# Hybrid decoder layer on one core: the input projection in chunks of 2, 3, 5 and 6 k-tiles, its last chunk in 24 blocks of two tiles, and more sums by transfers

## The chip, the cores and the metric

The kernel is one program on one core of a Trainium2 chip. Its time is the device time of one execution in microseconds, the median of three runs. The engines are named as the profile names them: PE multiplies, DVE and ACT do elementwise work, POOL here mostly issues transfers, and SP issues the loads of weights. [...]

## The reference, cut to what matters

```python
mod = (silu(c) @ w_mod + b_mod)                      # 6 vectors of 2048
h = rmsnorm(x, mix_pre_w) * (1 + sc_m) + sh_m        # x: 256 x 2048, float32
proj = h @ w_in                                      # 2048 x 6160: cb, cc, cx, q, k, v, r, a_lr
y_conv = cb * causal_dwconv3(cc * cx, conv_w)
o = gla_chunked(q, k, v, log_sigmoid(a_lr @ gate_w2 + gate_b) / 16)
y_gla = rmsnorm(o, gla_norm_w) * silu(r)
x = x + g_m * rmsnorm(concat(y_conv, y_gla) @ w_out, mix_post_w)
h = rmsnorm(x, ffn_pre_w) * (1 + sc_f) + sh_f
x = x + g_f * rmsnorm((silu(g) * val) @ w_down, ffn_post_w)   # g, val = split(conv3(h @ w_up))
```

All is float32 and nothing is kept from an earlier call: every weight, w_mod's 100 MB among them, is read once per execution.

## The kernel before

Each weight comes from memory as float32 into one of six `raw` tiles (`NRAW`). ACT copies it to the matmul's type (`wh`, L140) and DVE subtracts that from the original (`wl`, L145), so a product is the sum of three matmuls: high by high, high by low and low by high. There are three buffers each of `wh` and `wl`.

The input projection (`in_units`) goes over the 16 k-tiles of h in four chunks, `CHUNKS = (2, 4, 5, 5)`, because h needs the modulation vectors sc_m and sh_m, which are themselves a product with w_mod that DVE makes row by row (`mod_steps`: one L136 per k-row of w_mod, into an accumulator). While chunk i is multiplied, the modulation of chunk i+1's k-tiles is loaded and accumulated. Each chunk goes over all 48 output tiles of 128 columns in units: four tiles a unit in chunks 0 and 1, mostly three in chunks 2 and 3. Tiles 0 to 23 are cb, cc and cx, 24 to 31 are q and k, 32 to 39 v and 40 to 47 r. Tiles from 32 on (`mm_rows`, L602 to L604) have h as the loaded operand and the weights as the streamed one, the others (`mm`, L638 to L640) the reverse. Some pairs of tiles stay in PSUM from one chunk into the next (`keep`); for the others each chunk adds its part to a sum in SBUF: `evac` and `evac_rows`, a DVE addition (L477, L494) or, in the last chunk and for the names in `BY_DMA`, an ACT copy into one of three `hf` tiles (`NHF`) and then a transfer issued by POOL that adds to its destination (L475, L492).

`drive` sets the order. For unit i it issues: its `early` steps, the load and the ACT copy of unit i+2 (`prep`), the DVE subtraction of unit i+1 (`low`), the `pre` steps, the matmuls (`inner` steps between), `mid` steps, the sums of unit i-1 (`fin`, one unit late), and the `late` steps. Tables say at which unit a step goes: `MODS` the ends of the stretches over which the modulation steps are spread, `CONV`, `SILU` and `GATE` the places of the convolution, of silu(r) and of the gating. The gated linear attention of q, k and v runs inside the last chunk: nine levels (`gla_level`), one a unit from `G0` on, each with DVE differences (L763), ACT exponentials (L782, L783), DVE products (L799), PE score products (L737) and masked copies by DVE or ACT (L820, L818); then `gla_out` multiplies by v (L839 to L842), takes norms on ACT (L401), scales (L861), multiplies by silu(r) (`gated`, L868), turns the result on PE (`turn`, L874) and splits it (`weighted`, L880, and `weighted_low`). `tail` is the list of the last chunk's units followed by the 16 units of the output projection (`out_units`, 24 matmuls of 512 columns in most), whose first four units use the convolution's half and the next four the attention's.

After that come the feed-forward's two projections, which the change leaves as they are.

Of the kernel before, what the change touches and what calls it, by code (L numbers as in the profile page):

```python
# [21 lines left out]
HEADS = 4  # L22
TAU = 16.0
QS = 128.0 ** -0.5
CHUNKS = (2, 4, 5, 5)
PLAIN = ()
NMASK = 6
XRE = 5
NA = 10
G0 = 3  # L30
SQ = 1
LEAD = 2
S0 = 61
# [2 lines left out]
NBIG = 20  # L36
XLD = (4, 8)
NLD = (9, 13)
GATE = (18, 19, 20, 21)
SILU = (17, 18)  # L40
CONV = (9, 12, 13, 15)
MODS = (10, 22, 33, 48, 72)
CHUNK1 = 12
BUSY_TAIL = (12, 13, 16, 17)
BY_DMA = ("cc", "cx", "v")
F2_AT = (71, 74, 16)
FULL = ()
FULL1 = ()
FULL2 = ()
# [18 lines left out]
def spread(steps, units, last=()):  # L68

    places = [p for u in units for p in ((u.early, u.mid, u.late) if u in last else (u.early, u.mid))]  # L70
    for i, f in enumerate(steps):
        places[i * len(places) // len(steps)].append(f)
# [31 lines left out]
def layer_kernel(ctx: ExitStack, tc, x, c, w_mod, b_mod, mix_pre_w, mix_post_w, w_in, conv_w, gate_w2, gate_b,  # L104
# [14 lines left out]
    def nm(s):  # L119
        uid[0] += 1  # L120
        return f"{s}_{uid[0]}"

    def slot(shape, dt=F32):
        return big.tile(shape, dt, tag="big", name=nm("big"))
# [7 lines left out]
    def raw_tile(shape):  # L132
        return wts.tile(shape, F32, tag="raw", name=nm("raw"), bufs=NRAW)

    def stt(o, a, s, b, op0=ALU.mult, op1=ALU.add):
        nc.vector.scalar_tensor_tensor(o, a, s, b, op0=op0, op1=op1)  # L136
# [24 lines left out]
    def mod_steps(s0, n, a, w, nj, lag=0):  # L161

        accs, cur, rows = [], {}, []

        def use(j, r):
            stt(cur["acc"], r, c_act[:, j:j + 1], cur["acc"])

        def begin():  # L170
            acc = cur["acc"] = (slot([P, n, w]) if n * w <= 1024 else
                                wts.tile([P, n, w], F32, tag="macc", name=nm("macc"), bufs=2))
            accs.extend(acc[:, s, :] for s in range(n))
            nc.gpsimd.memset(acc, 0.0)
            nc.gpsimd.dma_start(acc[0:1, :, :], b_mod_v[:, s0:s0 + n, a:a + w])

        def step(j):
            if j >= KT:
                use(*rows.pop(0))
                return  # L180
            m = nj if j < KT - nj or nj < 4 else 2
            if j % m == 0:
                cur["r"] = raw_tile([P, m, n, w])
                if m == 1:
                    nc.sync.dma_start(cur["r"][:, 0, :, :], w_mod_v[:, j, s0:s0 + n, a:a + w])
                else:
                    for s in range(n):
                        nc.sync.dma_start(cur["r"][:, :, s, :], w_mod_v[:, j:j + m, s0 + s, a:a + w])
            rows.append((j, cur["r"][:, j % m, :, :]))
            if j >= lag:  # L190
                use(*rows.pop(0))

        return accs, [begin] + [lambda j=j: step(j) for j in range(KT + lag)]

    W0 = CHUNKS[0] * P
    first_acc = slot([P, 2, W0])
# [259 lines left out]
    hts, h32 = {}, {}  # L456
    hf0 = slot([P, CHUNKS[0], T])

    written, left = set(), {}

    def evac(ci, pair, ps):

        name = names[pair // 2]
        if name not in proj:
            proj[name] = slot([P, 4, T])
        dst = proj[name][:, (pair % 2) * 2:(pair % 2) * 2 + 2, :]
        if pair not in written:
            written.add(pair)
            nc.scalar.activation(dst, ps, AF.Copy, scale=QS if name == "q" else 1.0)
        elif name == "q":  # L470
            stt(dst, ps, QS, dst)
        elif ci == len(CHUNKS) - 1 and name[:-1] in BY_DMA and pair != 10:
            away_sum = hf_tile()
            nc.scalar.copy(away_sum, ps)
            nc.gpsimd.dma_start(dst, away_sum, accum_op=ALU.add)  # L475
        else:
            nc.vector.tensor_add(dst, dst, ps)  # L477

    def evac_rows(ci, tiles, t, ps):
# [7 lines left out]
        if ci == 0:  # L487
            nc.scalar.copy(dst, ps)
        elif ci == len(CHUNKS) - 1 and name[:-1] in BY_DMA:
            away_sum = hf_tile().rearrange("p a t -> p (a t)")[:, :w]  # L490
# [5 lines left out]
    def modulate_chunk(ci, ash, early=None):  # L496
# [4 lines left out]
        def at_once():  # L501

            n = CHUNKS[0]
            for kts in pairs(k0, k1):
# [50 lines left out]
    def in_units(ci):  # L555
        k0, n = bounds[ci], CHUNKS[ci]
        if ci == 0:
            groups = [tuple(range(g, g + 4)) for g in list(range(0, 24, 4)) + list(range(44, 20, -4))]
        elif ci == 1:
            groups = [tuple(range(g, g + 4)) for g in list(range(24, 48, 4)) + list(range(0, 24, 4))]  # L560
        elif ci == 2:
            groups = [tuple(range(g, g + 3)) for g in range(21, -1, -3)]
            groups += [(45, 46, 47), (42, 43, 44), (40, 41), (37, 38, 39), (34, 35, 36), (32, 33), (30, 31)]
            groups += [tuple(range(g, g + 3)) for g in (27, 24)]
        else:
            groups = [(24, 25, 26), (27, 28, 29), (30, 31), (32, 33, 34), (35, 36, 37), (38, 39)]
            for o, m in ((0, 3), (3, 3), (6, 2)):
                groups += [tuple(range(g + o, g + o + m)) for g in (8, 16, 0)]
            groups += [(40, 41, 42), (43, 44, 45), (46, 47)]

        keep = ((12, 13, 14, 15), (8, 9, 10, 11), (12, 13, 14), ())[ci]
        banks, done, begun, more = {}, {}, {}, {}
# [1 line left out]
        def unit(tiles, plain, by_parts=False):  # L574
# [72 lines left out]
            def fin():  # L647
                for p in dict.fromkeys(nt // 2 for nt in tiles):
                    done[p] = done.get(p, 0) + sum(nt // 2 == p for nt in tiles)
                    if done[p] == 2 and p not in keep:  # L650
                        evac(ci, p, banks[p])
# [238 lines left out]
    def gate_silu(g):  # L890
        for t in range(2):
            r = proj[f"r{t}"][:, g * 512:(g + 1) * 512]
            nc.scalar.activation(r, r, AF.Silu)
# [273 lines left out]
    for j in range(12, KT, 2):  # L1167
        first_load(j, 2, slot)
    load_small()
    chunks = [in_units(ci) for ci in range(len(CHUNKS))]  # L1170
    e = CHUNKS[0] * P
    rs = {}
# [34 lines left out]
    ash, products, columns = mod_columns([first_acc[:, i, :] for i in range(2)], CHUNKS[0], pre_c[:, :CHUNKS[0]], "ash0")  # L1207
# [17 lines left out]
    allin = [u for c in chunks for u in c] + owait  # L1225
# [4 lines left out]
    for ci in range(1, len(CHUNKS)):  # L1230
        n, us = CHUNKS[ci], chunks[ci - 1]
        st = {}
        st["accs"], steps = mod_steps(0, 2, bounds[ci] * P, n * P, 2 if n <= 4 else 1, 1)
        spread(steps, allin[CHUNK1 if ci == 2 else at:MODS[ci - 1]], [c[-1] for c in chunks])
        at = MODS[ci - 1]

# [15 lines left out]
    tail = chunks[-1] + owait  # L1252
    gacc, gsteps = mod_steps(2, 1, 0, 2048, 1)
    spread(gsteps, [u for i, u in enumerate(allin) if at <= i < MODS[3]], [c[-1] for c in chunks])
    load, ones_rows, rows_used = mod_rows(gacc, mix_post_w, lambda: [slot([P, 1024]) for _ in range(2)])
    r0 = 2
    owait[r0].late.append(load)
    for h in range(2):
        owait[r0 + R0 + 1].mid.append(lambda h=h, f=ones_rows: f(h))
        owait[r0 + R0 + 2].late.append(lambda h=h, f=rows_used: f(h))  # L1260
    f1, fsteps = mod_steps(3, 2, 0, 1024, 1)
    spread(fsteps, [u for i, u in enumerate(allin) if MODS[3] <= i < MODS[4] and i - ends[2] not in BUSY_TAIL])
    for place, f in seconds:
        place.append(f)
# [14 lines left out]
    levels = [-1, 0, 1, 2, 3, 4, 5, 6, 7]  # L1279
    tail[3].late.append(gla_s)  # L1280
    for i, lv in enumerate(levels):
        diff, decay, mult, products, put = gla_level(lv)
        if lv >= 0:
            tail[G0 + i].late.append(diff)
            tail[G0 + i + 1].early.append(decay)
            tail[G0 + i + 1].pre.append(mult)
        tail[G0 + i + 2].inner.append(products)
        tail[G0 + i + 2].late.append(put)
    outputs, norms, scaled, gated, turn, weighted, weighted_low = gla_out()
    GO = G0 + len(levels) + 3  # L1290
    tail[GO].early.append(outputs)
    tail[GO].late.append(norms)
    tail[GO + 1].pre.append(scaled)
    for g in range(2):
        tail[SILU[g]].late.append(lambda g=g: gate_silu(g))
    for e in range(4):
        tail[GATE[e]].pre.append(lambda e=e: gated(e))
        tail[GATE[e]].late.append(lambda e=e: turn(e))
        tail[GATE[e] + 1].pre.append(lambda e=e: weighted(e))
        tail[GATE[e] + 1].late.append(lambda e=e: weighted_low(e))  # L1300
    for i, u in enumerate(CONV):
        first, tap, second, high_part, third = conv_pair(i)
# [244 lines left out]
```

## Time and profile before

| | us |
|---|---|
| median of three runs | 1202.89 (1202.86 to 1203.3) |
| profiled execution, its own time | 1203.08 |
| its span, first to last instruction | 1201.1 |
| PE busy | 1166.5 |
| DVE busy | 939.5 |
| ACT busy | 576.7 |
| first matmul of chunk 0 / 1 / 2 / 3 | 26.0 / 68.7 / 142.9 / 232.9 |
| first matmul of the output projection | 344.7 |

The span is what the trace covers; the execution's own time lies 2.0 us above it. The granted clock of PE is 0.998 over the span. A matmul's end is modelled in this trace and overlaps the next one, so PE's pace is read from the distance between two starts. The rows by line mix several instructions that a helper issues: L136 is every scalar-times-tensor-plus-tensor, and the tiles tell them apart (`macc<-raw,c_act,macc` is a modulation row).

### The profile page before, as it was taken

What the parts mean: (1) busy time and instruction counts of PE and PEld (TensorE: products, weight loads), DVE (VectorE), ACT (ScalarE), POOL (GpSimd) and SP (SyncE); (2) the same over time, 40 slices, a digit from 0 to 9 for tenths busy, and PEclk for the clock granted to TensorE, in tenths of its full rate; (3) what the DMA queues carried; (4) which work ended last, traced back from release to release, by engine and by line L of the source; (5) the groups of instructions that cost most, each with busy time, mean ns of one, the idle gap of its engine ahead of it and who ended that gap; (6) DMA issues with size and microseconds to landing.
All of it is one profiled execution on the core that took longest, in us unless ns stands there. A gap on an engine that the chain in (4) does not pass through costs nothing.

```text
span 1201.1 us, 16724 instructions
## 1 busy us (share of the span) xinstructions
PE 1166.5 (97%) x6771; PEld 1027.6 (86%) x6771; DVE 939.5 (78%) x963; ACT 576.7 (48%) x671; POOL 47.8 (4%) x66
## 2 busy tenths in 40 slices
PE   3899999999999999999999999999999999999997
PEld 2799999999987888888888888888888888888885
DVE  6979999999999868984698979797976664545463
ACT  4663433463683556445455444544544544343442
POOL 3000110011101010000000000000000000000000
PEclk9999999999999999999999999999999999999999
DMA  9999999998899969995476777668563675555522
GB/s 340 387 361 378 331 383 393 388 330 272 240 341 372 367 248 333 378 369 212 168 260 213 258 259 249 223 243 293 201 236 140 228 263 201 185 202 184 207 73 71
DMA packets 129182, 323.62 MB, mean 269 GB/s; under 512 B 8550, under 2 KB 35894, under 8 KB 119377
## 3 DMA queue, kind: packets, MB, share of 16 engines
q1 hardware_dynamic: 124704, 312.63, 72.2%
q0 software_dynamic: 4256, 9.92, 3.0%
q8 instruction: 53, 0.87, 0.3%
q14 instruction: 25, 0.20, 0.0%
q10 hardware_dynamic: 144, 0.01, 0.0%
HBM read 315.45 MB, written 4.19 MB: 266 GB/s over the span
## 4 chain that ended last, share of the span: by engine, by line
PE 57%; issue 30%; DVE 5%; DMA 5%; ACT 1%; SPq 1%; POOL 1%; POOLq 0%; DVEq 0%; ACTq 0%
PE ps L1057 27%; PE ps L1059 14%; PE ps L913 3%; PE ps L915 3%; PE ps L914 3%; DVE wl L145 1%; DMA big<-hf 1%; PE ps L640 1%; PE ps L639 1%; DVE macc L136 1%; PE ps L638 1%; DMA raw<-in_w_mod_dram 1%; DMA big<-in_w_in_dram 1%; DMA raw<-in_w_in_dram 1%; DMA big<-in_w_mod_dram 1%
## 5 line engine op out<-in xcount | busy, mean ns | idle before, releaser
L140 ACT CAST wh<-raw 128x2048 fp32r<-128x2048 f32 (+2 forms) x200 | 366.3, 1833 | 498.3 <-PE ps L1057 187.3
L145 DVE TENSOR_TENSOR wl<-raw,wh 128x2048 fp32r<-128x2048 f32 (+2 forms) x200 | 437.4, 2190 | 144.7 <-ACT wh L140 144.6
L1057 PE MATMUL ps<-big,wh 128*128 128x512 f32 x1400 | 495.0, 399 | 0.0
L1059 PE MATMUL ps<-big,wl 128*128 128x256 f32 x1400 | 393.1, 281 | 0.0
L1057 PEld LDWEIGHTS ps<-big,wh 128*128 128x128 f32 x1400 | 263.0, 188 | 64.8
L1059 PEld LDWEIGHTS ps<-big,wl 128*128 128x128 f32 x1400 | 264.5, 189 | 0.0
L136 DVE SCALAR_TENSOR_TENSOR macc<-raw,c_act,macc 128x2048 f32<-128x2048 f32 (+1 forms) x96 | 199.3, 2076 | 4.5 <-DMA raw<-in_w_mod_dram 2.2
L913 PE MATMUL ps<-wh,big 128*128 128x512 f32 x456 | 178.4, 391 | 0.0
L915 PE MATMUL ps<-wh,big 128*128 128x512 f32 x456 | 177.5, 389 | 0.0
L914 PE MATMUL ps<-wl,big 128*128 128x512 f32 x456 | 177.5, 389 | 0.0
L640 PE MATMUL ps<-big,wl 128*128 128x256 f32 x504 | 143.3, 284 | 4.6 <-DVE wl L145 4.6
L638 PE MATMUL ps<-big,wh 128*128 128x256 f32 x504 | 143.8, 285 | 0.0
L639 PE MATMUL ps<-big,wh 128*128 128x256 f32 x504 | 142.6, 283 | 0.1
L640 PEld LDWEIGHTS ps<-big,wl 128*128 128x128 f32 x504 | 96.5, 192 | 5.9 <-DVE wl L145 5.8
L915 PEld LDWEIGHTS ps<-wh,big 128*128 128x128 f32 x456 | 85.6, 188 | 18.0
L913 PEld LDWEIGHTS ps<-wh,big 128*128 128x128 f32 x456 | 85.6, 188 | 17.9 <-issue 0.2
L914 PEld LDWEIGHTS ps<-wl,big 128*128 128x128 f32 x456 | 85.6, 188 | 17.6 <-issue 0.2
L639 PEld LDWEIGHTS ps<-big,wh 128*128 128x128 f32 x504 | 96.6, 192 | 0.3 <-DVE big L433 0.3
L638 PEld LDWEIGHTS ps<-big,wh 128*128 128x128 f32 x504 | 96.6, 192 | 0.4 <-ACT wh L140 0.3
L136 DVE SCALAR_TENSOR_TENSOR big<-big,fcw,big 128x254 f32<-128x254 f32 (+1 forms) x176 | 72.1, 475 | 0.0
L983 DVE TENSOR_TENSOR big<-big,ps 128x256 f32<-128x256 f32 x88 | 31.1, 415 | 46.5 <-ACT big L981 46.5
L604 PE MATMUL ps<-wl,big 128*128 128x384 f32 (+2 forms) x168 | 57.1, 340 | 1.2 <-DVE wl L145 1.2
(222 smaller groups left out, 914.0 us busy)
## 6 DMA issues: line engine op xcount, KB each, us to landing
raw<-in_w_up_dram SPq DMA_DIRECT2D x88, 1024.0 KB, 5.1
raw<-in_w_mod_dram SPq DMA_DIRECT2D x64, 1024.0 KB, 6.9
raw<-in_w_down_dram SPq DMA_DIRECT2D x44, 1024.0 KB, 4.8
raw<-in_w_in_dram SPq DMA_DIRECT2D x26, 960.0 KB, 8.0
raw<-in_w_mod_dram SPq DMA_DIRECT2D x32, 640.0 KB, 7.9
raw<-in_w_out_dram SPq DMA_DIRECT2D x16, 1024.0 KB, 7.5
raw<-in_w_in_dram SPq DMA_DIRECT2D x12, 1024.0 KB, 9.1
raw<-in_w_mod_dram SPq DMA_DIRECT2D x22, 512.0 KB, 8.4
```

Source lines behind the costliest of these rows:

```text
L136: nc.vector.scalar_tensor_tensor(o, a, s, b, op0=op0, op1=op1)
L140: nc.scalar.copy(hi, raw)
L145: nc.vector.tensor_sub(lo, raw, hi.bitcast(F32))
L604: nc.tensor.matmul(ps, ht[:, 0, :], w[1][:, kk, :], start=False, stop=kk == n - 1)
L638: nc.tensor.matmul(ps, w[0][:, kk, cs], ht[:, k % 2, 0, :], start=st, stop=False)
L639: nc.tensor.matmul(ps, w[0][:, kk, cs], ht[:, k % 2, 1, :], start=False, stop=False)
L640: nc.tensor.matmul(ps, w[1][:, kk, cs], ht[:, k % 2, 0, :], start=False, stop=sp)
L913: nc.tensor.matmul(ps, a[:, i, 0, ts_], w[0][:, kk, ns], start=st, stop=False)
L914: nc.tensor.matmul(ps, a[:, i, 0, ts_], w[1][:, kk, ns], start=False, stop=False)
L915: nc.tensor.matmul(ps, a[:, i, 1, ts_], w[0][:, kk, ns], start=False, stop=sp)
L1057: nc.tensor.matmul(pss[o], wh[:, kk, cs], h2[k // 2][:, k % 2, :, :], start=(first and kk == 0), stop=False)
L1059: nc.tensor.matmul(pss[o][:, 1, :], wl[:, kk, cs], h2[k // 2][:, k % 2, 0, :], start=False, stop=(last and kk == 3))
```

## The change

- `CHUNKS` becomes (2, 3, 5, 6). The modulation of chunk 1 covers three k-tiles instead of four, that of chunk 3 six instead of five.
- The last chunk goes in 24 units of two tiles (`groups`) instead of 18 units of three or two. Its order is the same: q, k and v, then cc, cx and cb by turns, then r.
- `LEVEL_AT` gives each attention level its own unit; mostly every second unit takes one. `G0` goes.
- `BY_DMA` takes cb and r too, and the exception for pair 10 goes: all sums of the last chunk except q and k go by transfer. These are 12 transfers of 256 KB and 16 of 128 KB, where there were 7, and 6 of 192 or 128 KB.
- `CONV`, `SILU`, `GATE`, `MODS`, `BUSY_TAIL` and `F2_AT` move with the units.
- The first step of the feed-forward's modulation (a memset and a small load on POOL, `f_begin`) goes two units ahead of the others.

```diff
-CHUNKS = (2, 4, 5, 5)
+CHUNKS = (2, 3, 5, 6)
-G0 = 3
-GATE = (18, 19, 20, 21)
-SILU = (17, 18)
-CONV = (9, 12, 13, 15)
-MODS = (10, 22, 33, 48, 72)
+GATE = (24, 25, 26, 27)
+SILU = (23, 24)
+CONV = (12, 15, 18, 21)
+MODS = (10, 22, 33, 50, 78)
-BUSY_TAIL = (12, 13, 16, 17)
-BY_DMA = ("cc", "cx", "v")
-F2_AT = (71, 74, 16)
+BUSY_TAIL = (13, 15, 17, 19, 22, 23)
+BY_DMA = ("cb", "cc", "cx", "v", "r")
+F2_AT = (77, 80, 16)
+LEVEL_AT = (3, 5, 7, 9, 11, 12, 14, 16, 18)
...
-        elif ci == len(CHUNKS) - 1 and name[:-1] in BY_DMA and pair != 10:
+        elif ci == len(CHUNKS) - 1 and name[:-1] in BY_DMA:
...
-            groups = [(24, 25, 26), (27, 28, 29), (30, 31), (32, 33, 34), (35, 36, 37), (38, 39)]
-            for o, m in ((0, 3), (3, 3), (6, 2)):
-                groups += [tuple(range(g + o, g + o + m)) for g in (8, 16, 0)]
-            groups += [(40, 41, 42), (43, 44, 45), (46, 47)]
+            firsts = list(range(24, 40, 2))
+            for o in range(0, 8, 2):
+                firsts += [g + o for g in (8, 16, 0)]
+            groups = [(g, g + 1) for g in firsts + list(range(40, 48, 2))]
...
-    f1, fsteps = mod_steps(3, 2, 0, 1024, 1)
+    f1, (f_begin, *fsteps) = mod_steps(3, 2, 0, 1024, 1)
+    allin[MODS[3] - 2].late.append(f_begin)
...
-            tail[G0 + i].late.append(diff)
-            tail[G0 + i + 1].early.append(decay)
-            tail[G0 + i + 1].pre.append(mult)
-        tail[G0 + i + 2].inner.append(products)
-        tail[G0 + i + 2].late.append(put)
+            tail[LEVEL_AT[i]].late.append(diff)
+            tail[LEVEL_AT[i] + 1].early.append(decay)
+            tail[LEVEL_AT[i] + 1].pre.append(mult)
+        tail[LEVEL_AT[i] + 2].inner.append(products)
+        tail[LEVEL_AT[i] + 2].late.append(put)
...
-    GO = G0 + len(levels) + 3
+    GO = LEVEL_AT[-1] + 3
```

Three places show what moves. The first is SP in the second half of chunk 0: its own weights (`in_w_in`, 2 k-tiles by 512 columns) between the modulation rows of chunk 1. Before, and then in the changed kernel:

```order
L585 DMA raw_422<-in_w_in_dram 128x2x512
L188 DMA raw_458<-in_w_mod_dram 128x2x512 x2
L585 DMA raw_462<-in_w_in_dram 128x2x512
L188 DMA raw_486<-in_w_mod_dram 128x2x512 x2
L585 DMA raw_490<-in_w_in_dram 128x2x512
```

```order
L585 DMA raw_422<-in_w_in_dram 128x2x512
L188 DMA raw_458<-in_w_mod_dram 128x2x384 x2
L585 DMA raw_462<-in_w_in_dram 128x2x512
L188 DMA raw_486<-in_w_mod_dram 128x2x384 x2
L585 DMA raw_490<-in_w_in_dram 128x2x512
```

The order is the same; the modulation rows have 384 columns instead of 512.

The second is ACT from the scaling of the attention's result to the third `wh` of the output projection, with the semaphores that each row waits for (`DMASW` counts POOL's transfers, `DMAHW` SP's loads; `big_511` and `big_513` are r, the first and the second 128 rows of it). Before:

```order
L861 ACTIVATE big_3401<-ps_3323,grs 128x256 x2
L684 CAST big_3445<-big_337 128x2x256 [waits DVE_49]
L140 CAST wh_3449<-raw_3447 128x2048 [waits DMAHW1_49,PE_49]
L893 ACT_TABLE_LOAD
L893 ACTIVATE big_511<-big_511 128x512 [waits DVE_49]
L893 ACTIVATE big_513<-big_513 128x512 [waits DVE_49]
L140 CAST wh_3495<-raw_3493 128x2048 [waits DMAHW3_49,PE_49]
L893 ACTIVATE big_511<-big_511 128x512 [waits DVE_49]
L893 ACTIVATE big_513<-big_513 128x512 [waits DVE_49]
L140 CAST wh_3543<-raw_3541 128x2048 [waits DMAHW5_49,PE_49,Activation_49]
```

And in the changed kernel:

```order
L491 COPY hf_3589<-ps_3464 128x256 [waits DMASW2_49]
L491 COPY hf_3592<-ps_3483 128x256 [waits DMASW3_49,PE_49]
L684 CAST big_3595<-big_337 128x2x256 [waits DVE_49]
L140 CAST wh_3599<-raw_3597 128x2048 [waits DMAHW1_49,PE_49]
L491 COPY hf_3641<-ps_3551 128x256 [waits DMASW4_49]
L491 COPY hf_3644<-ps_3570 128x256 [waits DMASW5_49,PE_49,Activation_49]
L893 ACT_TABLE_LOAD
L893 ACTIVATE big_511<-big_511 128x512
L893 ACTIVATE big_513<-big_513 128x512 [waits DMASW6_49]
L140 CAST wh_3652<-raw_3650 128x2048 [waits DMAHW2_49,PE_49]
L491 COPY hf_3689<-ps_3603 128x256 [waits Activation_49]
L491 COPY hf_3692<-ps_3622 128x256 [waits DMASW7_49,PE_49,Activation_49]
L893 ACTIVATE big_511<-big_511 128x512 [waits DMASW1_49]
L893 ACTIVATE big_513<-big_513 128x512 [waits DMASW2_49,DMASW0_49]
L140 CAST wh_3704<-raw_3702 128x2048 [waits DMAHW4_49,DVE_49,PE_49]
```

The four silu rows waited for DVE's additions; now copies for r stand between them, and they wait for POOL's transfers.

The third is DVE at the second and third unit of the output projection in the changed kernel (`big_3708` is the first turned piece that `weighted_low` splits, L868 is `gated`):

```order
L145 TENSOR_TENSOR wl_3706<-raw_3650,wh_3652 128x2048
L868 TENSOR_TENSOR big_3536<-big_3536,big_511 128x256
L868 TENSOR_TENSOR big_3541<-big_3541,big_513 128x256
L136 SCALAR_TENSOR_TENSOR big_3708<-ps_3697,sv,big_3708 128x256 x2
L136 SCALAR_TENSOR_TENSOR macc_2655<-raw_3744,c_act,macc_2655 128x2048
L145 TENSOR_TENSOR wl_3751<-raw_3702,wh_3704 128x2048
L868 TENSOR_TENSOR big_3536<-big_3536,big_511 128x256
```

The last row, `gated` for the third piece, stands behind a `wl` whose `wh` (`wh_3704`) is the last ACT row shown above; that part of DVE's order is as it was.

## The prediction

> **What bounds the kernel now.** I read the busy times by stage first: chunk 0, 1, 2 and 3 of the input projection, and the output projection. Columns: PE, weight loads, DVE, ACT, POOL, clock, DMA share, GB/s.
>
> ```profile
> core 0: us, PE busy (x) PEld busy (x) DVE busy (x) ACT busy (x) POOL busy (x), PEclk, DMA share, GB/s
> 26.00:68.70 42.70, 38.81 (x264) 34.55 (x265) 37.33 (x34) 30.17 (x43) 0.00 (x0) 1.00 1.05 387
> 68.70:142.90 74.20, 74.12 (x535) 69.83 (x534) 68.64 (x56) 32.11 (x28) 2.04 (x4) 1.00 0.99 354
> 142.90:232.90 90.00, 90.00 (x703) 89.93 (x701) 87.62 (x71) 32.95 (x26) 8.08 (x4) 1.00 1.04 387
> 232.90:344.70 111.80, 109.29 (x831) 106.91 (x830) 107.16 (x113) 65.27 (x107) 14.76 (x17) 1.00 0.92 295
> 344.70:440.00 95.30, 94.85 (x428) 76.91 (x427) 83.22 (x71) 43.79 (x50) 3.19 (x3) 1.00 0.94 355
> ```
>
> PE never stops for long, yet DVE is nearly as full from 69 to 345: 263.4 of 276 us. Chunk 0 alone has PE idle, and there the loads run at 387 GB/s. The change ends before 440, so at most some ten us of PE idling are to be won. Next, PE's waits, in chunk 0 (first two rows) and from 233 to 360:
>
> ```profile
> PE ps L640 <- DVE wl L145: 2.2, 2, 1.7
> PE ps L604 <- DVE wl L145: 1.2, 2, 0.6
> ...
> PE ps L640 <- DVE wl L145: 2.4, 2, 1.9
> PE ps L874 <- DVE big L868: 0.4, 1, 0.4
> ```
>
> Each is a wait for the low half of a weight, except the last (`turn` for `gated`). A wait shows less than it costs: a matmul's modelled end lies 0.28 us behind its start, and the next starts 0.12 us later.
>
> ```profile
> 265.17 0.28 PE L638 MATMUL ps<-big,wh 128*128 128x256 f32 x1
> 265.29 0.28 PE L639 MATMUL ps<-big,wh 128*128 128x256 f32 x1
> ...
> 340.15 0.33 PE L602 MATMUL ps<-wh,big 128*128 128x384 f32 x1
> 340.32 0.33 PE L603 MATMUL ps<-wh,big 128*128 128x384 f32 x1
> ...
> 344.68 0.40 PE L913 MATMUL ps<-wh,big 128*128 128x512 f32 x1
> 344.91 0.40 PE L914 MATMUL ps<-wl,big 128*128 128x512 f32 x1
> ```
>
> By starts and counts, PE's own work is 36.5 us of chunk 0's 42.7 (8 units of 24 matmuls at 0.12, 4 of 12 at 0.23, products and transposes 2.6), 107.4 of chunk 3's 111.8 (five k-tiles 85.4, 136 score products 15.2, the product with v and the gate 6.8), and nearly all of chunks 1 and 2.
>
> **The change, chunk by chunk.** A k-tile costs PE 48 x 3 x 0.12 = 17.3 us; one moves from chunk 1 to chunk 3. Narrow rows are near free: three matmuls of 256 take 0.36 us, two of 384 0.34, some 0.8 us in all.
>
> Chunk 0. Its low halves come late because the loads do:
>
> ```profile
> ACT wh L140 <- DMA raw<-in_w_in_dram: 4.8, 2, 2.8
> ...
> raw<-in_w_mod_dram SPq DMA_DIRECT2D x22, 512.0 KB, 8.4
> ```
>
> Sixteen of these 22 loads are chunk 1's modulation, 0.5 MB each; three k-tiles instead of four take away 2.1 MB, 5.4 us at 387 GB/s. The last weights of chunk 0 then land that much earlier and PE paces the chunk: 35.8 us of work (0.7 less, a tile's products and transposes) and 1.0 us of starting waits. Chunk 1 starts at 62.8 instead of 68.7: **-5.9**.
>
> Chunk 1. DVE's prices:
>
> ```profile
> L145 DVE TENSOR_TENSOR wl<-raw,wh 128x2048 fp32r<-128x2048 f32 x29 | 66.1, 2284 | 11.4 <-ACT wh L140 11.4
> L145 DVE TENSOR_TENSOR wl<-raw,wh 128x1920 fp32r<-128x1920 f32 x26 | 55.9, 2150 | 1.9 <-ACT wh L140 1.8
> L145 DVE TENSOR_TENSOR wl<-raw,wh 128x1280 fp32r<-128x1280 f32 x9 | 13.3, 1483 | 0.5 <-ACT wh L140 0.5
> L136 DVE SCALAR_TENSOR_TENSOR macc<-raw,c_act,macc 128x2048 f32<-128x2048 f32 x34 | 79.7, 2344 | 2.7 <-issue 2.2 <-DMA raw<-in_w_mod_dram 0.5
> L136 DVE SCALAR_TENSOR_TENSOR macc<-raw,c_act,macc 128x1280 f32<-128x1280 f32 x32 | 49.3, 1540 | 1.8 <-DMA raw<-in_w_mod_dram 1.7
> L477 DVE TENSOR_TENSOR big<-big,ps 128x512 f32<-128x512 f32 x28 | 18.2, 674 | 0.4 <-PE ps L640 0.4
> ...
> 341.15 1.01 DVE L494 TENSOR_TENSOR big<-big,ps 128x384 f32<-128x384 f32 x2
> L494 DVE TENSOR_TENSOR big<-big,ps 128x384 f32<-128x384 f32 x12 | 6.1, 548 | 0.0
> ```
>
> The last two rows say that neighbours overlap by 0.08 us (2 x 0.548 against 1.01), which I take off per instruction. A low half of 1536 columns, new, lies between 1.48 and 2.15; by the line through them 1.75. The chunk's list: 12 low halves 21.0, 16 modulation rows of 1280 24.6, one of 1536 (1.81 by the same line) 1.8, 16 additions 10.8, small ones 2.2, less 51 x 0.08: 56.2 us. PE needs 56.5 (74.2 - 17.3 within 0.4). Before, the same sum is 62.7 against 74.2, so DVE ran ahead. Now it has no margin, and its idle time counts (68.64 busy of 74.2: 5.6 us, mostly waits for ACT after the new h and for one raw load); I take 4.5, since loads shrink: 60.7 us, **+3.8** against PE's need of 56.9. Bounds: 56.5, PE alone, and 65.
>
> Chunk 2. Modulation rows grow from 1280 to 1536 columns, 16 x 0.27 = 4.3 us, and one row of 2048 moves on, -2.3: DVE 89.6, with the 2.4 of idle that the stage has now 92.0. PE: 90.0 + 0.7. **+2.0**; bounds +0.7 and +5, the upper for loads, which ran at 387 GB/s here already and have 2.1 MB more.
>
> Chunk 3. PE: 107.4 + 17.3 + 0.8 = 125.5. DVE: 107.2; low halves +6.8 (24 x 1.75 for 12 x 2.15 + 6 x 1.48, less overlaps); five additions of 0.67 and three of 0.55 gone, -4.3; four more modulation rows in the stretch, +9.0; together 119, with the idle of now (4.6) 123.3. The attention's levels at every second unit and the earlier `f_begin` (its wait is the 2.2 "issue" above) keep work from bunching, but the two engines are nearly equal, so I add 1.5 to PE's: 127, against 111.8 + 17.3: **-2.1**. Bounds -3.7 and +2. POOL has 28 transfers of some 0.9 us, hidden by 127 us of chunk; conv's sums have about two units of 5 us before their readers, more than a landing (below). Output projection starts at 342.5 instead of 344.7: **-2.2** so far.
>
> **The sums of r.** Here the transfers meet a reader at once. Their time from issue to landing (min, median, max), POOL's time for one issue (three figures in ns), the median for r's size, and ACT's and DVE's prices:
>
> ```profile
> DMA to landing us min/median/max: 3.9/7.0/9.4
> L492 POOL DMA_DIRECT2D big<-hf x6: 852/895/1247, 257.1 to 274.2; - x6
> ...
> big<-hf POOLq DMA_DIRECT2D x2, 128.0 KB, 7.1
> ...
> L401 ACT ACTIVATE junk<-ps 128x256 bf16<-128x256 f32 x8 | 3.1, 383 | 0.2
> L851 ACT ACT_TABLE_LOAD x1 | 1.3, 1283 | 0.0
> L861 ACT ACTIVATE big<-ps,grs 128x256 f32<-128x256 f32 x8 | 3.0, 478 | 0.0
> L491 ACT COPY hf<-ps 128x256 f32<-128x256 f32 x2 | 0.7, 362 | 3.5 <-DMA big<-hf 3.5
> L893 ACT ACTIVATE big<-big 128x512 f32<-128x512 f32 x4 | 2.3, 624 | 1.7 <-DVE big L494 1.7
> L880 ACT ACTIVATE big<-ps,sv 128x256 fp32r<-128x256 f32 x8 | 3.3, 469 | 0.0
> L140 ACT CAST wh<-raw 128x2048 fp32r<-128x2048 f32 x7 | 13.4, 1911 | 8.7 <-issue 5.5 <-PE ps L915 3.2
> L868 DVE TENSOR_TENSOR big<-big,big 128x256 f32<-128x256 f32 x8 | 3.0, 420 | 0.0
> ```
>
> Take T as the end of attention's product with v; then PE has three units (13.0 us) before the output projection, whose units take 5.5 us and 0.5 for `turn`. ACT after T: the last square sums, a table load and a root to T+3.0, conv's taps 3.9, `wh` once a buffer is free 6.3, eight scalings 9.3, then two copies of r (9.6, 10.0), which POOL issues at 9.7 and 10.6. With 7.0 they land at 16.7 and 17.6. The fourth copy in turn has no `hf` tile until 16.7; then the table load (18.4) and two silus (19.6). `gated`, 2 x 0.42, ends at 20.4; PE wants to turn at 13.0 + 5.5: 2.0 late. Behind the silus on ACT stand the next `wh` (21.5) and the last two copies of r (22.1), and the next two silus wait for those very sums: issued at 21.9 and 22.8. By then few weights have been freed to load, so I take a landing of 5.5, between 3.9 and 7.0: 28.3, silus 28.9, `wh` 30.8, `weighted` 31.6. DVE holds its order: `weighted_low` 32.4, a modulation row 34.7, `wl` 36.9, `gated` 37.7. PE is done with the third unit at 32.4: 5.4 late. Together **+7.5**, of which the 0.8 that `turn` cost before (0.4 seen, twice 0.16 hidden) goes off: +6.7. With landings of 3.9 both times the delay is 2.8, with 9.4 13. From there PE has what it had; the rest is unchanged.
>
> The Trainium skill, "DMA: Bandwidth & Descriptors", section "Anatomy of one DMA — SWDGE (gpsimd) path", gives a transfer issued by GpSimd 2.0 us plus its bytes at 436 GB/s, an estimate of 2.3 us for 128 KB. The rows here, 3.9 at least under a loaded DMA, disagree. By the rule the third `gated` would come 0.4 late and the sum be 1202.9 - 2.2 - 0.4 = 1200.3.
>
> Sum: 1203.08 - 2.2 + 6.7 = 1207.6 for the profiled execution; the median lies 0.2 below, so **1207.4**.
>
> **Rivals.** (1) *Sums land soon.* If the transfers land in the 3.9 us of the quickest one, PE is late by 2.8 rather than 7.5: 1202.9 - 2.2 + 2.0 = 1202.7, no change. For it: DMA is freer once ACT stalls. Against: the median for 128 KB is 7.1. With landings of 2 us, half the quickest row, nothing is late and the old 0.8 goes too: 1202.9 - 2.2 - 0.8 = 1199.9, faster. That is the side on which the page's rule stands.
>
> (2) *PE paces every chunk.* If DVE's idle time was slack that it could afford, chunks 1 to 3 take PE's 56.5, 90.7 and 125.5: the projection starts at 62.8 + 272.7 = 335.5, 9.2 earlier, and 1202.9 - 9.2 + 6.7 = 1200.4, faster. For it: no PE wait at all from 69 to 233 before. Against: DVE's lists equal PE's within 0.3 us in chunk 1.
>
> (3) *DVE and loads starve.* Each DVE idle keeps `raw` tiles longer, loads come later, and the idle of chunks 1 and 2 doubles, +7 against my sum: 1214. For it: both engines and the loads are all full there. Against: loads now stay back to back from 142.9 to 232.9 with DVE at 97%.
>
> **How the numbers follow.** Forecast 0.57; rival 1 0.11 with landings of 3.9 and 0.05 with 2; rival 2 0.12; rival 3 0.15. Range: the bottom takes in rivals 1 and 2, 1199.8; the top lies between the forecast and rival 3, 1212.8. About 0.2%, 2.4 us, is what a measurement here can tell: faster 0.05 + 0.12 = 0.17; same 0.11 and 0.13 of the forecast, where its terms fall small, 0.24; slower 0.44 + 0.15 = 0.59.
>
> **What would show it.** Chunk 1's first matmul near 62.8; chunk 1 lasting 60 to 61 with PE waits for L145, none of which stood there before; chunk 3's near 215.5; the output projection's near 342.5. Then ACT's L893 waiting for a transfer `big<-hf`, some 6 us in the second pair, and PE's L874 waiting for DVE L868 by 7 to 8 us in all. I am wrong if the silus wait little, or if chunk 1 lasts under 58.

## The result

The changed kernel takes 1214.7 us (median of four, 1213.45 to 1215.06) where the kernel before takes 1202.88 (1202.64 to 1203.3): a ratio of 1.0097, 95% interval 1.0082 to 1.0111, 11.8 us slower. The forecast was 1207.4 with a range up to 1212.8: the direction was right, the size too small.

First the busy times by stage of the changed kernel (chunk 0, 1, 2, 3, output projection), as the prediction showed them of the kernel before:

```profile
core 0: us, PE busy (x) PEld busy (x) DVE busy (x) ACT busy (x) POOL busy (x), PEclk, DMA share, GB/s
25.70:62.90 37.20, 36.77 (x259) 34.10 (x259) 32.89 (x35) 29.50 (x43) 0.00 (x0) 1.00 1.06 381
62.90:125.40 62.50, 58.06 (x413) 53.61 (x412) 60.20 (x55) 25.60 (x26) 2.04 (x4) 1.00 1.01 362
125.40:216.80 91.40, 91.20 (x709) 90.79 (x709) 91.22 (x71) 34.24 (x27) 6.05 (x4) 1.00 1.05 388
216.80:347.20 130.40, 126.59 (x1034) 124.92 (x1033) 118.60 (x116) 77.18 (x125) 23.35 (x27) 1.00 1.02 323
347.20:440.70 93.50, 87.17 (x386) 70.50 (x384) 70.19 (x51) 40.06 (x42) 7.48 (x9) 0.96 0.90 327
```

Two stages have PE idle where the kernel before had hardly any: chunk 1 (4.4 us) and the output projection (6.3 us, and the mean clock is 0.96 there). Chunk 3 has 3.8 us of it, in two waits, at 268 and 274.5 us, where the kernel before had 2.5. PE's waits in these three stages, one after the other (us in total, times, longest):

```profile
PE ps L640 <- DVE wl L145: 4.1, 4, 1.5
...
PE ps L640 <- DVE wl L145: 3.8, 2, 2.1
...
PE ps L874 <- DVE big L868: 6.3, 1, 6.3
```

By the first matmul of each stage, the two profiled executions stand so (us):

| | before | changed | length before | length changed | predicted |
|---|---|---|---|---|---|
| chunk 0 | 26.0 | 25.7 | | | |
| chunk 1 | 68.7 | 62.9 | 74.1 | 62.5 | 60.7 |
| chunk 2 | 142.9 | 125.4 | 90.0 | 91.5 | 92.0 |
| chunk 3 | 232.9 | 216.8 | 111.8 | 130.4 | 127 |
| output projection | 344.7 | 347.2 | 86.4 to its last unit | 93.5 | +6.7 |
| last unit of it | 431.0 | 440.7 | | | |
| last matmul of all | 1192.3 | 1202.0 | | | |
| end of span | 1201.1 | 1211.7 | 8.7 | 9.7 | 0 |

So 2.5 us are lost by the start of the output projection, 7.1 more in it, nothing in the 760 us of the feed-forward, and 1.0 behind the last matmul: 10.6, the difference of the spans. The profiled execution is the shortest of the four; the median lies 1.25 above it.

**The output projection.** DVE ahead of the wait, and PE behind it (start, duration, instruction, in brackets the idle time before it and what ended it); then the granted clock in four stretches:

```profile
365.24 0.88 DVE L136 SCALAR_TENSOR_TENSOR big<-ps,sv,big 128x256 fp32r<-128x256 f32 x2 [7.60 <-ACT big L880]
366.03 2.34 DVE L136 SCALAR_TENSOR_TENSOR macc<-raw,c_act,macc 128x2048 f32<-128x2048 f32 x1
368.29 2.29 DVE L145 TENSOR_TENSOR wl<-raw,wh 128x2048 fp32r<-128x2048 f32 x1
370.49 0.76 DVE L868 TENSOR_TENSOR big<-big,big 128x256 f32<-128x256 f32 x2
...
371.06 1.14 PE L874 MATMUL ps<-ident,big 128*128 128x128 f32 x4 [6.33 <-DVE big L868]
371.85 0.77 PE L913 MATMUL ps<-wh,big 128*128 128x512 f32 x1
372.43 0.63 PE L914 MATMUL ps<-wl,big 128*128 128x512 f32 x1
372.85 0.63 PE L915 MATMUL ps<-wh,big 128*128 128x512 f32 x1
```

```profile
360.00:366.00 6.00, 4.73 (x21) 3.57 (x19) 0.76 (x2) 4.59 (x6) 0.00 (x0) 1.00 1.06 391
366.00:371.00 5.00, 0.00 (x0) 0.00 (x0) 5.00 (x5) 3.52 (x4) 0.00 (x0) 0.63 0.30 86
371.00:372.40 1.40, 1.34 (x5) 1.22 (x6) 1.40 (x4) 0.16 (x1) 0.00 (x0) 0.50 1.02 418
372.40:374.10 1.70, 1.70 (x5) 1.32 (x4) 1.70 (x1) 0.68 (x2) 0.00 (x0) 0.50 1.06 422
```

PE wants the third turned piece at 364.6 and gets it at 371.06. Then its matmuls of 512 columns start 0.42 us apart instead of 0.23, and until 374.1 the granted clock is 0.50. The third unit of the output projection lasts 12.9 us and the fourth 7.0, against 5.94 each without the wait: 8.0 us. What DVE waited for is told by ACT and by the transfers that POOL issued from the second pair of copies:

```profile
353.75 0.63 ACT L491 COPY hf<-ps 128x256 f32<-128x256 f32 x2
360.88 0.63 ACT L893 ACTIVATE big<-big 128x512 f32<-128x512 f32 x1 [6.51 <-DMA big<-hf]
362.04 0.63 ACT L893 ACTIVATE big<-big 128x512 f32<-128x512 f32 x1 [0.52 <-DMA big<-hf]
362.58 1.89 ACT L140 CAST wh<-raw 128x2048 fp32r<-128x2048 f32 x1
364.38 0.83 ACT L880 ACTIVATE big<-ps,sv 128x256 fp32r<-128x256 f32 x2
```

```profile
DMA to landing us min/median/max: 6.5/6.7/7.0
```

The second pair of silus waits 6.5 us for sums issued at 354.4 and 354.9; behind them on ACT stand `wh` and `weighted`, behind these on DVE `weighted_low`, a modulation row and `wl`, and only then `gated`.

**Chunk 3.** DVE (first two rows) stands still once, for 4.76 us, in front of the first modulation row of the feed-forward; below it what POOL did in that time:

```profile
259.84 1.28 DVE L799 TENSOR_TENSOR big<-big,big 128x512 f32<-128x512 f32 x2
265.88 2.35 DVE L136 SCALAR_TENSOR_TENSOR macc<-raw,c_act,macc 128x2048 f32<-128x2048 f32 x1 [4.76 <-issue]
...
257.92 0.85 POOL L492 DMA_DIRECT2D big<-hf  x1 [3.99 <-ACT hf L491]
258.45 2.14 POOL L174 MEMSET macc<- 128x2048 f32 x1
260.89 0.55 POOL L175 DMA_DIRECT2D macc<-in_b_mod_dram  x1 [0.30 <-POOL macc L174]
```

The memset and the small load of `f_begin` stand in POOL's queue behind a transfer of v's sums that waited 4 us for ACT's copy. The load goes out at 260.9 and lands 4.9 us later; the row, which adds to what was loaded, begins at 265.9.

### The profile page after: what moved, and what is told of

Its sections match the earlier page's. It is cut to its first block, busy times and chain, and to the rows that moved or that the text cites. A ratio compares the mean times of both kernels' runs of the same rounds, so it can differ in the third digit from the quotient of the medians.

```text
span 1211.7 us, 16972 instructions
## 1 busy us (share of the span) xinstructions
PE 1168.2 (96%) x6855; PEld 1030.8 (85%) x6855; DVE 935.5 (77%) x958; ACT 582.9 (48%) x692; POOL 58.6 (5%) x81
## 3 DMA queue, kind: packets, MB, share of 16 engines
q0 software_dynamic: 6416, 12.28, 4.2%
## 4 chain that ended last, share of the span: by engine, by line
PE 77%; issue 7%; DVE 7%; DMA 5%; POOL 1%; ACT 1%; SPq 1%; DVEq 0%; POOLq 0%; ACTq 0%
PE ps L1057 27%; PE ps L1059 14%; PE ps L915 9%; PE ps L913 9%; PE ps L914 9%; DVE wl L145 3%; DVE macc L136 2%; PE ps L604 1%; DMA raw<-in_w_in_dram 1%; PE ps L602 1%; PE ps L603 1%; PE ps L638 1%; PE ps L639 1%; PE ps L640 1%; DMA big<-hf 1%
## 5 line engine op out<-in xcount | busy, mean ns | idle before, releaser
L140 ACT CAST wh<-raw 128x2048 fp32r<-128x2048 f32 (+3 forms) x206 | 367.3, 1785 | 492.1 <-PE ps L1057 187.3
L145 DVE TENSOR_TENSOR wl<-raw,wh 128x2048 fp32r<-128x2048 f32 (+3 forms) x206 | 438.4, 2131 | 146.9 <-ACT wh L140 146.8
L136 DVE SCALAR_TENSOR_TENSOR macc<-raw,c_act,macc 128x2048 f32<-128x2048 f32 (+2 forms) x96 | 203.8, 2123 | 6.1 <-issue 4.8
L604 PE MATMUL ps<-wl,big 128*128 128x256 f32 (+2 forms) x196 | 62.1, 317 | 0.8 <-DVE wl L145 0.8
```

Of the source, the lines that this page charges most:

```text
L140: nc.scalar.copy(hi, raw)
L145: nc.vector.tensor_sub(lo, raw, hi.bitcast(F32))
L604: nc.tensor.matmul(ps, ht[:, 0, :], w[1][:, kk, :], start=False, stop=kk == n - 1)
```

## The experiments

The theory after the traces: three separate losses, one in chunk 1 (DVE or the loads), one of 4 us in chunk 3 (POOL's queue) and one of 8 us in the output projection (r's transfers and what queues behind them). Each run is compared with the kernel before on the same chip.

**r summed by DVE again**

```diff
-BY_DMA = ("cb", "cc", "cx", "v", "r")
+BY_DMA = ("cb", "cc", "cx", "v")
```

> The changed kernel with the last sums of r back on DVE (eight additions of 128x256 instead of eight transfers); nothing else differs. Theory A, the transfers of r are what stops PE at 371 us: the silus no longer wait for landings, PE's 6.5 us wait for the third gated product goes, and the half clock of the 3 us behind it too, 8.1 us in all; eight additions of about 0.35 us give DVE 3 us more, in a stage where it has room: 1214.7 - 8 = 1206 to 1207.5. Rival B, the wait at 371 is DVE's order (its list of low half, modulation row and gated product) and would stand without transfers: 1213 to 1216.

Measured: 1205.37 us (1204.21 to 1208.22), ratio to before 1.0025 [1.0015, 1.0034]: 9.3 us off. In the output projection PE waits for nothing of DVE any more, and the third and fourth unit take 5.94 us each. Theory A holds, and the gain is a little more than it said. Of the 1.3 us beyond its 8, 0.65 is at the end of the program (9.0 us from the last matmul on instead of 9.7; see the last section); the rest no trace places.

**The modulation sum begun four blocks earlier**

```diff
-    allin[MODS[3] - 2].late.append(f_begin)
+    allin[MODS[3] - 6].late.append(f_begin)
```

> The changed kernel with the start of the first of the two last modulation sums (a memset and a load of 16 KB on POOL) four blocks earlier, ahead of v's transfers in POOL's queue. Theory A, DVE's idle 4.8 us at 261 to 266 us is its first modulation row waiting for that load, which stood behind v's transfers: the idle time goes, PE's waits at 270 and 276 (2.24 and 1.89) too, and the output projection starts 4 us earlier; what the transfers of r cost stays: 1210 to 1211.5. Rival B, DVE and PE are so near equal in this chunk that the time comes back as other waits for low halves: 1213.5 to 1215.

Measured: 1210.04 (1209.56 to 1212.07), ratio 1.0063 [1.0048, 1.0078]: 4.7 us off. (The load that was moved is of 8 KB, not 16.) The same place on DVE has no gap:

```profile
259.93 1.28 DVE L799 TENSOR_TENSOR big<-big,big 128x512 f32<-128x512 f32 x2
261.13 2.33 DVE L136 SCALAR_TENSOR_TENSOR macc<-raw,c_act,macc 128x2048 f32<-128x2048 f32 x1
```

Chunk 3 takes 126.1 us, 0.6 above PE's own 125.5, and PE waits for nothing in it. Theory A holds. The change had moved this step two blocks ahead of its row; it needed to be ahead of v's transfers, of which there are eight now instead of six.

**Both**

> Both edits at once: r summed by DVE and the modulation sum begun four blocks earlier. If the two costs are apart, as theory A has it, they add: 8 and 4 us off 1214.7, 1202 to 1204, level with the kernel before. If an earlier output projection only meets its weights later (rival B), less than 10 us come off: above 1205.

Measured: 1201.0 (1200.34 to 1202.95, ten executions) against 1202.77 for the kernel before, measured beside it: ratio 0.9986 [0.9977, 0.9996]. The two gains, 9.3 and 4.7, add to 14.0; both together give 13.7, a little below the 1202 to 1204 that were expected. They are separate. This is the quickest kernel of the study, 1.8 us under the kernel before, though less than the 2.4 us that a measurement here can tell.

**The old split with everything else mended**

```diff
-CHUNKS = (2, 3, 5, 6)
+CHUNKS = (2, 4, 5, 5)
```

> The changed kernel with both mends (r summed by DVE, the modulation sum begun four blocks earlier) and the old chunks of 2, 4, 5 and 5 k-tiles; the 24 blocks of two tiles, the spread attention and the other sums by transfers stay. Against the kernel with both mends, 1201.0. Theory A, the split pays nothing: chunk 0 ends 5.9 later (68.7), chunk 1 takes 74.2, chunk 2 90.0 and chunk 3, at PE's pace, 126 - 17.3 = 108.7, so that the output projection starts near 341.6 instead of 343.8, and the time is 1198 to 1200. Rival B, the split is what takes DVE's load off: chunk 3 stays DVE's at 111 or more and the time is 1201 to 1204.

Measured: 1206.14 (1205.51 to 1207.77), ratio to before 1.0025 [1.0015, 1.0035]: 5.1 us above the kernel with both mends. The time lies above both ranges: theory A fails, and rival B's side is right by more than it said. Chunk 3, then PE's waits in it:

```profile
232.50:350.20 117.70, 111.80 (x890) 109.33 (x889) 112.90 (x120) 70.89 (x120) 18.43 (x22) 0.99 1.01 319
```

```profile
PE ps L640 <- DVE wl L145: 5.3, 4, 1.7
```

With five k-tiles PE needs 108 us there and DVE has 112.9 us of work, more than the 107.2 before: fifteen modulation rows of 2048 columns fall into the chunk instead of twelve (7.0 us). Besides, a standstill of 1.7 us at 305 is followed by 3.4 us at a clock of 0.50. A sixth k-tile brings PE 17.3 us of work, and the chunk is longer by 8.4 only (126.1 with both mends and the new split). So the split does pay here, and the 24 blocks with their steps and transfers, without it, cost 3.2 us against the kernel before.

**Half of chunk 1's sums by transfers too**

```diff
-        elif ci == len(CHUNKS) - 1 and name[:-1] in BY_DMA:
+        elif ci == 1 and pair % 2 or ci == len(CHUNKS) - 1 and name[:-1] in BY_DMA:
...
-        elif ci == len(CHUNKS) - 1 and name[:-1] in BY_DMA:
+        elif ci == 1 and t or ci == len(CHUNKS) - 1 and name[:-1] in BY_DMA:
```

> The changed kernel, with half of the sums of the second chunk of the projection (eight of 128x512) also made by transfers, whose readers come a chunk later. Theory A, DVE paces that chunk (PE waits 5.2 us for low halves in it, DVE has no idle time from 79 to 125 us): eight additions less, 8 x 0.59 = 4.7 us, take 3.5 to 5 us off, chunk 2 starts near 121: 1210 to 1211.5. Rival B, the loads pace it: eight transfers of 256 KB take their share of the DMA, 5 us at 387 GB/s, and the chunk gets no shorter or longer: 1214 to 1219.

Measured: 1225.15 (1224.23 to 1227.07), ratio 1.0187 [1.0172, 1.0202]: 10.5 us above the changed kernel, worse than rival B said; chunk 1 took 69.6 us. DVE's rows and ACT's h in that stage, with the idle time before them and what ended it:

```profile
L136 DVE SCALAR_TENSOR_TENSOR macc<-raw,c_act,macc 128x1280 f32<-128x1280 f32 (+1 forms) x18 | 28.4, 1576 | 11.7 <-DMA raw<-in_w_mod_dram 6.2 <-DMA macc<-in_b_mod_dram 5.4
...
L420 ACT ACTIVATE hf<-ps,ash 128x256 f32<-128x256 f32 x6 | 3.2, 562 | 4.8 <-DMA big<-hf 3.8 <-PE ps L414 1.0
```

DVE waited 6.2 us for loads; 5.4 us for the first small load of the next modulation sum, again behind transfers in POOL's queue; and ACT 3.8 us for an `hf` tile still being read. It left theory A open, since DVE's sums, the loads and POOL's queue all changed at once. The next three runs take work away instead of moving it.

**Chunk 1 without half of its sums; without half of its modulation loads; without both**

```diff
+        elif ci == 1 and pair % 2:
+            pass
...
+        elif ci == 1 and t:
+            pass
```

```diff
-            if j % m == 0:
+            if j % m == 0 and not (w == 640 and j % 2):
```

> The changed kernel with half of the sums of the second chunk (eight additions of 128x512 on DVE) left out, so its output is not the reference's; no transfer takes their place. Theory A, DVE paces chunk 1: 4.7 us less on DVE take 3.5 to 5 us off the chunk (62.5 to 57.5 to 59, PE alone 56.5), and 1214.7 becomes 1210 to 1211.5. Rival B, the loads pace it (raw tiles come back no faster, as they come late): DVE's 4.7 us turn into idle time before low halves and modulation rows, the chunk stays above 61, and the time at 1213 to 1215.

> The changed kernel, in whose second chunk every other load of a modulation row (640 KB each) is left out and the row before used twice, so that the output is not the reference's; DVE's and PE's instructions stay as they are. Theory B, after the run without half of the sums: the loads pace chunk 1. Eight loads less, 5.2 MB or 13.8 us at the 380 GB/s of this stretch, leave DVE's list (56.2) and PE (56.5) as the bound: the chunk takes 57 to 60 instead of 62.5, the whole 2.5 to 5 us less, 1209.5 to 1212. Theory A, DVE paces it: 61.5 to 62.5 as before, 1214 to 1215.5.

> The changed kernel with both cuts in chunk 1: half of its sums left out (as in the run without half of the sums) and every other load of a modulation row left out (as in the run with half of the loads); the output is not the reference's. Theory C, two bounds lie so close together that taking off either one alone shows the other: with both off PE alone paces the chunk, 56.5 to 58 us instead of 62.5, 61.9 and 61.1, and the whole is 4.5 to 6 us under the changed kernel, 1208.5 to 1210.5. Theory D, something third paces it (ACT's high halves, the order of the loads): 60 us or more, 1211 or more.

Measured: without the sums 1215.22 (two executions), ratio 1.0098 [1.008, 1.0116]; without the loads 1211.88 (two), 1.0072 [1.0052, 1.0092]; without both 1210.43 (three), 1.0065 [1.0042, 1.0088]. Chunk 1 took 62.5 us in the changed kernel, then 61.9, 61.1 and 57.9. The modulation rows of chunk 1 in the changed kernel and in these three runs, in this order:

```profile
L136 DVE SCALAR_TENSOR_TENSOR macc<-raw,c_act,macc 128x1280 f32<-128x1280 f32 (+1 forms) x19 | 30.0, 1582 | 1.3 <-DMA raw<-in_w_mod_dram 1.3
```

```profile
L136 DVE SCALAR_TENSOR_TENSOR macc<-raw,c_act,macc 128x1280 f32<-128x1280 f32 (+1 forms) x19 | 30.2, 1587 | 4.2 <-DMA raw<-in_w_mod_dram 4.1
```

```profile
L136 DVE SCALAR_TENSOR_TENSOR macc<-raw,c_act,macc 128x1280 f32<-128x1280 f32 (+1 forms) x18 | 28.2, 1569 | 0.1
```

```profile
L136 DVE SCALAR_TENSOR_TENSOR macc<-raw,c_act,macc 128x1280 f32<-128x1280 f32 (+1 forms) x19 | 30.1, 1582 | 0.1
```

With less to do DVE waits for loads (4.1 us); with fewer loads its modulation rows have no wait left and it is itself late, so that PE waits 1.2 us at each of three blocks; with both cut the chunk is within 1.4 us of PE's own 56.5. Either cut alone takes off 0.5 or 1.4 us, both 4.6. Theory C holds: two limits lie close together. Theory A and theory B, one limit alone, do not fit the chunk's length after each cut. This rests on one trace each; the whole times, of two or three executions, agree but for the first, which did not get shorter.

**The modulation rows of chunk 2 begun earlier, with both mends**

```diff
-CHUNK1 = 12
+CHUNK1 = 10
```

> The kernel with both mends (1201.0), with the modulation rows for chunk 2 begun at block 10 instead of 12, so that two or three of their sixteen loads and products go into the end of chunk 0. If the loads of chunk 1 bunch (theory B), 1.3 to 1.9 MB less in it is 3 to 5 us at 380 GB/s, of which chunk 0 gives back up to 2: 1197.5 to 1200. If chunk 0 is as full as chunk 1 (its loads run at 380 GB/s too), the first weights of chunk 1 come later by what is won: 1200.5 to 1203.

> The same with the rows begun at block 11: one load or two go ahead of chunk 1. Theory B: 1199 to 1200.5; chunk 0 as full as chunk 1: 1200.5 to 1202.

Measured: from block 10 1201.33 (1200.33 to 1202.15), ratio 0.9986 [0.9976, 0.9995]; from block 11 1202.61 (1200.5 to 1203.69), 0.9993 [0.9983, 1.0002]. Neither is better than the 1201.0 without it. From block 10 chunk 0 takes 37.3 us instead of 36.7, and chunk 1 62.5 instead of 63.2: what the one gains the other gives back.

**PE kept busy in the wait**

```diff
             st[e2] = ps = bank([P, 2, T])
+            if e2 == 2:
+                for _ in range(20):
+                    nc.tensor.matmul(ps, ones_r, owait[2].weights()[:, 0, :512], start=True, stop=True)
...
```

> The changed kernel with 20 idle matmuls of 512 columns (4.6 us) put on PE just ahead of the third turn, while it waits for the gated product. Theory A, the half clock of 371 to 374 us follows from PE's standstill: with PE busy until about 370.7 the clock stays at 1.00 and 1.4 to 1.8 us come off: 1213. Rival B, the clock falls for another reason, or the matmuls behind the wait were slow for their weights: 1214 to 1215.

Measured: 1213.52 (1211.58 to 1215.88), ratio 1.0085 [1.0071, 1.0099]. The 1.2 us off are within the spread of four executions, so the time does not decide; the clock does:

```profile
366.00:371.00 5.00, 3.40 (x16) 2.34 (x15) 5.00 (x5) 3.10 (x4) 0.00 (x0) 1.00 0.40 122
371.00:372.40 1.40, 1.40 (x9) 1.18 (x8) 1.40 (x3) 0.84 (x2) 0.00 (x0) 1.00 1.03 415
```

PE stands still for 1.6 us only, the clock stays at 1.00 here, and the fourth unit takes 5.92 us where it took 6.99: the half clock had cost 1.1 us there, and the third unit is 0.2 shorter. Theory A holds for the clock at this place; that a standstill of 1.6 us is short enough does not follow, as the last section shows from the same run.

**The second pair of silus a block later; then also the modulation sum begun earlier**

```diff
-SILU = (23, 24)
+SILU = (23, 25)
```

> The changed kernel with the second pair of silus one block later on ACT; r is still summed by transfers. Theory A, what cost 6.5 us was not the landing alone but what stood behind the two waiting silus on ACT and DVE (wh, the scaling, the low half, a modulation row, then the gated product): with wh ahead of them the silus end near 363, the gated product near 364, and PE, which wants it at 364.6, waits under 1 us: 1206 to 1208. Rival B, the landing itself decides: the product comes as late as before, 1213 to 1215.

> The changed kernel with the second pair of silus a block later and the modulation sum begun four blocks earlier; r is still summed by transfers. If the two costs are apart here too, 4.7 us come off the 1207.3 of the later silus: 1202.6, 1 to 2 us above the kernel that sums r on DVE (1201.0), since PE still waited 0.55 us in the output projection. If the transfers of r are worth something once nothing waits for them (3 us of DVE's time), it is below 1200.

Measured: 1207.29 (1205.31 to 1210.38), ratio 1.0035 [1.0024, 1.0046], and with the earlier start 1202.27 (1200.99 to 1204.96), 0.9993 [0.9984, 1.0002]. ACT in the first of them:

```profile
353.07 1.92 ACT L140 CAST wh<-raw 128x2048 fp32r<-128x2048 f32 x1
354.88 0.85 ACT L880 ACTIVATE big<-ps,sv 128x256 fp32r<-128x256 f32 x2
359.85 0.63 ACT L893 ACTIVATE big<-big 128x512 f32<-128x512 f32 x1 [4.12 <-DMA big<-hf]
361.03 0.63 ACT L893 ACTIVATE big<-big 128x512 f32<-128x512 f32 x1 [0.54 <-DMA big<-hf]
```

The transfers land no sooner (6.6 and 7.2 us after their issue), but `wh` and `weighted` are done before the silus wait, so `gated` starts at 361.6, and of the 8.0 us in the output projection 0.6 is left. So the landing alone was not what stopped PE: it was what the order put behind it. Even so the transfers of r are worth nothing: with the earlier start the time is 1.3 us above the kernel that sums r on DVE, of which 0.7 is in the fourth unit of the output projection and 0.6 behind the last matmul.

## Why the prediction failed on size

The forecast was 7.3 us short. The largest part, 3.4 us, is chunk 3, where a step that was to keep work from bunching made DVE stand still; chunk 1 and the end of the program follow.

**Chunk 0, right.** Chunk 1 was to start at 62.8 and started at 62.9.

**Chunk 1, mis-sized: +3.8 predicted, +5.6 measured.** The step was "56.2 of DVE's list plus 4.5 of idle". Both terms missed: DVE was busy for 60.2 us of the 62.5 and idle for 2.3, and that the sum came near was luck. The list was short already for the kernel before, 62.7 against the 68.64 of the window. In the changed kernel it counted one modulation row of 1536 columns, and there are three:

```profile
L136 DVE SCALAR_TENSOR_TENSOR macc<-raw,c_act,macc 128x1536 f32<-128x1536 f32 x3 | 5.4, 1799 | 0.0
```

These stand at the end, from 117.8 us on, behind PE's last wait. What held PE up stands in the middle, and a total for a chunk hides that: the modulation rows stand in ten of its twelve blocks and the sums in eight. From 79.5 us on DVE does not pause, and this is one of the middle blocks, from one low half to the next at 100.33:

```profile
94.54 1.74 DVE L145 TENSOR_TENSOR wl<-raw,wh 128x1536 fp32r<-128x1536 f32 x1
96.21 1.53 DVE L136 SCALAR_TENSOR_TENSOR macc<-raw,c_act,macc 128x1280 f32<-128x1280 f32 x1
97.67 1.27 DVE L494 TENSOR_TENSOR big<-big,ps 128x512 f32<-128x512 f32 x2
98.86 1.53 DVE L136 SCALAR_TENSOR_TENSOR macc<-raw,c_act,macc 128x1280 f32<-128x1280 f32 x1
```

That is 5.8 us where PE needs 4.3 (36 matmuls at 0.12). The loads, which I let shrink, were the second limit behind it.

**Chunk 2, about right.** +2.0 predicted, +1.5 measured; here too the list was short (91.2 us busy, not 89.6) and the idle time long (0.2, not 2.4).

**Chunk 3, the wrong step: "the earlier `f_begin` ... keep work from bunching" and "POOL has 28 transfers, hidden by 127 us of chunk".** POOL's time was hidden; its order was not. The transfers of v stood in front of `f_begin`, each waiting for a copy of ACT, and DVE's 2.2 us of idle, which the earlier step was to spare, became 4.8 and cost PE 3.8. With the step ahead of them the chunk takes 126.1, so PE's 125.5 and the 127 were sound.

**The sums of r, near in sum by luck, wrong in parts: +6.7 net predicted, 7.1 measured.** The first pair was to come 2.0 late and came in time: its transfers took 5.0 and 5.2 us instead of 7.0. The second was to come 5.4 late with a landing of 5.5, "by then few weights have been freed to load"; it came 6.5 late, with landings of 6.5 and 7.0, though the DMA was indeed almost idle when they were issued. The queue behind the silus was as drawn. Not in the sum at all: PE's clock after the standstill, 1.3 us by the run that kept PE busy (0.2 in the third unit, 1.1 in the fourth).

**The end, not in the sum: +1.0.** See the last section. These terms, 1.8 - 0.5 + 3.4 + 0.4 + 1.0, come to 6.1; the profiled execution's own time lies 0.2 less above its span than before; and the median lies 1.25 above it where I took it 0.2 below. That makes the 7.3 us by which the forecast was short.

**Of the rivals,** the first (transfers land soon) is refuted by 6.5 to 7.0 us, the second (PE paces every chunk) by chunk 1, and the third (DVE and loads starve, 1214) came nearest by its number and named chunk 1's two limits, but of the 7 us that it put into chunks 1 and 2 only 1.2 were there.

## What to carry to other kernels

A sum of work over a stage says whether it can fit, not whether it does: lay each engine's list against the pace block by block, with the depth of the buffers between. When work is moved to an engine that is nearly idle, read its queue in order: what else on it has a reader, and what does each entry wait for? And a result that comes late should be waited for by the last instruction that can wait, since everything that the order puts behind the waiter is late with it.

## What the runs showed of the hardware

**POOL's transfers cost time at the end of the program.** POOL begins to drain its queue beside its last instruction, at 1204.7 in the changed kernel, while outputs are still being stored (the last one is issued at 1206.5 and lands 3.0 us later); the end waits for both. The drains (ns, min/median/max, first and last start) in the kernel before, with both mends, in the changed kernel, and with eight more transfers in chunk 1:

```profile
L1531 POOLq DRAIN  x3: 46/93/4910, 1195.1 to 1200.8; - x3
```

```profile
L1532 POOLq DRAIN  x3: 46/93/5483, 1193.3 to 1199.3; - x3
```

```profile
L1532 POOLq DRAIN  x3: 46/102/6135, 1204.7 to 1211.4; - x3
```

```profile
L1532 POOLq DRAIN  x3: 51/93/6788, 1214.9 to 1222.2; - x3
```

POOL's own queue, q0 on the page, moved 4256, 5264, 6416 and 7568 packets in these four. The longest drain grows by 573 ns for 1008 packets, 652 for 1152 and 653 for 1152: 0.57 ns a packet each time, 0.08 us for a transfer of 144 packets, long after it has landed. The other eleven runs agree: 5478 to 5483 ns with 5264 packets, 6132 to 6137 with 6416. From the kernel before to the changed one that is 1.2 us, of which 1.0 shows in the span: before, the last output landed at 1199.9, as the drain ended at 1200.0, and now the drain ends 1.3 us behind the last landing. What the drain does is not in the trace.

**PE's clock falls after a standstill, but the length of it does not decide alone.** 6.3 us without a matmul left a granted clock of 0.50 until 3.0 us after PE went on; in the run that kept PE busy, 1.6 us left it at 1.00. But in chunk 3 of that same run 2.0 us without a matmul (first row) were followed by 0.50 for 3.4 us:

```profile
267.37:269.40 2.03, 0.00 (x1) 0.00 (x0) 2.03 (x3) 0.00 (x0) 0.00 (x0) 1.00 0.93 206
270.89:274.30 3.41, 3.41 (x18) 3.41 (x18) 3.41 (x3) 2.56 (x4) 0.00 (x0) 0.50 0.95 330
```

With the old split 1.7 us were enough, while 3.1 us (from 100.6, in the run with half of chunk 1's sums by transfers) left the clock at 1.00. Every stretch at 0.50 that ends before the last matmul lasted 3.4 us or two or three times that. The Trainium skill, "TensorE: Matmul & The Clock Gate", section "Part 1: The HAM clock gate (the "warmup" mystery)", gives windows of about 3.4 us of idling and of work for the fall and the return; the lengths of the stretches agree, but standstills of 1.7 and 2.0 us were enough for the fall here.

**Two adding transfers of 128 KB took 6.5 and 7.0 us, though the DMA was nearly idle when they were issued.** They are r's last two; from their issue, at 354.4 and 354.9, until 356.6 the DMA moved at most 94 GB/s:

```profile
GB/s 23 18 12 12 6 0 0 0 0 0 47 94 0 23 70 140 47 47 94 351 398 445 398 410 281 334 392 316 269 357 334 322 322 345 298 363 299 211 199 222
```

The row covers 354 to 361 us in forty slices. The first packet of the two moved at 358.1, 3.7 us after the first issue: from 354.9 to 358.0 there are 89 packets, all of SP's loads. The last packets moved at 361.4. So more than half of the first one's time had passed before any of it moved; whether the loads that set in at 357.3 stretched the rest, no run separates. The Trainium skill, "DMA: Bandwidth & Descriptors", section "Anatomy of one DMA — SWDGE (gpsimd) path", would make it 2.3 us, an estimate by its fit for one transfer; here no transfer of r in the changed kernel landed in under 3.6 us, so the trace disagrees.
